# Scaled, newly split input as 512 moving columns in three FFN up projections, with accumulators in pairs of banks

## The chip, the cores and the metric

The kernel runs on one core of one Trainium2 chip. The metric is device time of one execution in microseconds (us). Three runs of the kernel before gave 1129.79 to 1129.9 us, median 1129.81. The profiled execution took 1131.31 us, of which the trace shows a span of 1129.5 us at a mean granted TensorE clock of 0.992.

## The reference

One sequence of 256 tokens (T), width 1024 (D_MODEL), goes through three mixing layers, each followed by a convolutional feed-forward network (FFN). The first mixing layer has three branches (an RWKV-7 recurrence, stick-breaking attention, attention to a memory) that a gate joins; the second and the third are other mixers. All is fp32. The change lies in the FFN and in where every accumulator is put:

```python
def rms_norm(x, g, eps=NORM_EPS):
    xf = x.astype(jnp.float32)
    y = xf * lax.rsqrt(jnp.mean(xf * xf, axis=-1, keepdims=True) + eps)
    return (y * g.astype(jnp.float32)).astype(x.dtype)

def conv_ffn(x, g, w_up, conv_w, conv_b, w_down):
    h = rms_norm(x, g) @ w_up                      # 1024 -> 2 x 2816
    ...
    acc = conv_b + hp[:, 0:t] * conv_w[0]          # causal, 3 taps over time
    for i in range(1, CONV_W):
        acc = acc + hp[:, i:i + t] * conv_w[i]
    gate, val = jnp.split(acc, 2, axis=-1)
    return (jax.nn.silu(gate) * val) @ w_down      # 2816 -> 1024
```

## The kernel before

Channels lie on the 128 partitions and the 256 tokens on the free axis, so x is eight tiles of 128x256 (k = 0 to 7, KD = 8), kept in `xt`. An fp32 product is made from three float32r products: each operand is split into a high part (a rounded copy, made by ACT) and a low part (what is left, a subtraction by DVE), and hi x hi, hi x lo and lo x hi are summed in PSUM. `mm3` (L365 to L367) issues the three for one 128x128 weight block: weight hi with moving Xh, weight hi with Xl, weight lo with Xh, 256 columns each.

Weights stream in tiles of 1024 columns, eight blocks each: a DMA on SP's queue into `wstg`, an ACT copy into `whi` (L241), a DVE subtraction into `wlo` (L242), three buffers of each. This goes on through the whole kernel.

The FFN input is X2 (X4, X6 in the other two): x times the norm's gain, split, but not yet divided by each token's root mean square. That factor (`s_bc`, 128x256, one value for each token) comes late: PE sums the squares (`st_ps`, L462), DVE moves the sum (L464), GpSimd takes the inverse root in eleven steps (L406 to L418), PE spreads it over the partitions (`st_pb`, L472), and ACT copies it out of PSUM (L474). The order of tokens and channels lets it be applied to the product instead of the input.

An up projection has 22 pairs (NJ = 22) of half-tiles, one for the gate and one for the value; each half-tile takes eight blocks. The first HEAD = 4 half-tiles run in two rounds, k = 0 to 5 for all, then k = 6 and 7. The rest run one after the other. A pair's two halves fill one bank, 128x512. `evac` then has DVE multiply the bank by `s_bc` into one of three `ffu` buffers (L1123), makes the causal convolution on ACT (L1127) and DVE (L1128, L1129), silu on ACT (L1131), the product on DVE (L1132), and splits the result into Y[j] (`ffy`, high and low side by side; L339, L340).

The down projection (`residual`, L1077 to L1089) has one accumulator of 128x512 for each of eight output tiles m: weight hi with the 512 columns [Yh, Yl] (L1083), weight lo with the 256 of Yh (L1085), over 22 blocks, then two DVE additions into `xt` (L1087).

Accumulators come from `ps_acc`: four buffers of one bank (128x512 fp32) that go round under the tag "acc". Gates and branches of the first mixer use one such bank for each m, the gate in the first 256 columns and the branch in the other 256 (L1035 to L1053); ACT takes tanh of the gate (L1037), DVE joins it with the branch (L1048, L1050, L1051). The projections of the RWKV branch take token-shifted sums from such banks with an ACT copy (L603) and a DVE operation (L605).

A scheduler that works on the program decides the order of instructions on each engine and places the waits; a wait is for the instructions that last read or wrote the same tile. Stages, by time in the profiled execution: first mixer to 344.7 us (its output projection `XO`, L1056 to L1058, from about 321), first FFN up 344.7 to 472, down 472 to 534; second mixer to 639, its FFN up to 766, down to 830; third mixer to 935, its FFN up to 1064, down to the end.

Of the kernel before, what the change touches and what calls it, by code (L numbers as in the profile page):

```python
# [16 lines left out]
T = 256  # L17
# [8 lines left out]

STARTS = (82, 148, 181, 247, 279)
GRID = 4
HEAD = 4

# [162 lines left out]
def body(tc, a, out, voff, coff, tap=None, upto=99):  # L195
# [8 lines left out]
    dpool = es.enter_context(tc.tile_pool(name="dpool", bufs=1, space=bass.MemoryType.DRAM))  # L204
    psum = es.enter_context(tc.tile_pool(name="psum", bufs=1, space=PSUM))

    def ps_acc(name="acc"):
        return psum.tile([128, 512], F32, name=name, tag="acc", bufs=4)

    def ps_m(name="pm"):  # L210
        return psum.tile([128, 512], F32, name=name, tag="pm", bufs=2)
# [110 lines left out]
    def vec(n, k=0, w=1):  # L322
        o = voff[n][0] + k
        return vecs[:, o:o + w]
# [67 lines left out]
                flow.tick(4)  # L392

    def tp_group(X):
        po = [ps_acc(), ps_acc()]
        tp_groups(X, po)
        return po

# [656 lines left out]
    def residual(X, gains_next, snext, Xn, kn=KD, two=False):  # L1055
# [10 lines left out]
                snext.add(xt[:, m - 1:m + 1])  # L1066

        if two:
            ps = [ps_acc() for _ in range(4)]
            for kh in range(2):  # L1070
                for m in range(KD):
                    o = ps[m // 2][:, m % 2 * T:(m % 2 + 1) * T]
                    for k in range(4 * kh, 4 * kh + 4):
                        mm3(o, X, k, W.take(), k == 0 and m % 2 == 0, k == kn - 1, skip_group_check=True)
                    if kh == 1 and m % 2 == 1:
                        evac(m - 1, 2, ps[m // 2].rearrange("p (j t) -> p j t", t=T))
        elif isinstance(X, list):  # L1077

            for m in range(KD):
                ps = ps_acc()  # L1080
                for k in range(kn):
                    hi, lo = W.take()
                    PE.matmul(ps, hi, X[k].rearrange("p s t -> p (s t)"), start=(k == 0), stop=False,  # L1083
                              skip_group_check=True)
                    PE.matmul(ps[:, 0:T], lo, X[k][:, 0], start=False, stop=(k == kn - 1), skip_group_check=True)  # L1085
                for j in range(2):
                    V.tensor_tensor(xt[:, m], xt[:, m], ps[:, (1 - j) * T:(2 - j) * T], op=OP.add)  # L1087
                after_tile(m)
        else:  # L1089
# [12 lines left out]
    order.close()  # L1102
    mix.close()

    def ffn(X, st, cname, gains_next, snext, Xn_f):
        fs = ExitStack()
        fp = fs.enter_context(tc.tile_pool(name="ffn_" + cname, bufs=1))
        Y = []
# [8 lines left out]
            G.memset(u[:, :, 0:2], 0.0)  # L1117
            ub.append(u)

        def evac(i, m, ps2):  # L1120
            j = i // 2
            u = ub[j % 3]
            V.tensor_tensor(u[:, :, 2:], ps2, st.bc2, op=OP.mult)  # L1123
            ac = fp.tile([128, 2, T], F32, name="ffa", bufs=3)
            for g in range(2):
                c = (j * 2 + g) * 4
# [275 lines left out]
```

## Time and profile before

| | before |
|---|---|
| median of the runs | 1129.81 us (1129.79 to 1129.9) |
| profiled execution / span | 1131.31 / 1129.5 us |
| PE busy | 1102.4 us (98%) |
| DVE busy | 869.5 us (77%) |
| ACT busy | 664.3 us (59%) |
| GpSimd busy | 64.1 us (6%) |
| HBM read | 186.46 MB, 166 GB/s over the span |

Busy time is the union of an engine's instructions over the span. A matmul's own duration, 0.28 us for 256 columns, overlaps the next ones; what one costs in a row of them is the distance between two starts. "Idle before, releaser" at a row is how long its engine stood still ahead of it, and what it waited for. In a row of instructions a bracket such as [waits DVE_49] says that it waits for a semaphore of that engine.

### The profile page before, as it was taken

How to read it: one execution, taken by the hardware profiler on the slowest of the kernel's cores; microseconds unless marked ns; L12 is line 12 of the kernel's file. 1: busy time of each engine (PE TensorE's matmuls, PEld its weight loads, DVE VectorE, ACT ScalarE, POOL GpSimd, SP SyncE). 2: the span in 40 equal slices, each digit the busy share in tenths (PEclk: the TensorE clock that was granted, in tenths of full speed). 3: DMA queues.
4: the chain of work that ended last, by engine and by line, in shares of the span. 5: the costliest groups of instructions: out<-in, count | busy, mean ns of one | idle time of the engine just before them, and what ended most of it. 6: DMA issues, size and time to landing. Idle time of an engine off the chain costs nothing.

```text
span 1129.5 us, 21212 instructions
## 1 busy us (share of the span) xinstructions
PE 1102.4 (98%) x8266; PEld 1027.4 (91%) x8266; DVE 869.5 (77%) x1615; ACT 664.3 (59%) x1116; POOL 64.1 (6%) x167
## 2 busy tenths in 40 slices
PE   7999989999999999999999999999999999999998
PEld 4898769899999999988989999998888899999987
DVE  6669875667676999966656889997779768999854
ACT  6556546654555666645546666665555756666642
POOL 2100210000011000000100110000010002000000
PEclk9899999999999999999999999999999999999999
DMA  7444333335475555566554565565665536655573
GB/s 278 162 132 149 114 113 103 95 96 150 150 225 173 183 187 187 181 189 196 168 169 149 164 193 189 181 180 182 195 200 175 165 94 190 181 181 183 185 208 110
DMA packets 60788, 189.28 MB, mean 168 GB/s; under 512 B 12688, under 2 KB 14992, under 8 KB 60688
## 3 DMA queue, kind: packets, MB, share of 16 engines
q1 hardware_dynamic: 59792, 186.51, 53.2%
q8 instruction: 65, 1.06, 0.4%
q0 software_dynamic: 320, 1.05, 0.3%
q10 hardware_dynamic: 576, 0.37, 0.1%
q14 instruction: 35, 0.29, 0.1%
HBM read 186.46 MB, written 1.44 MB: 166 GB/s over the span
## 4 chain that ended last, share of the span: by engine, by line
PE 87%; DVE 4%; DMA 3%; ACT 2%; SPq 1%; issue 1%; POOL 0%; DVEq 0%; ACTq 0%
PE acc L365 18%; PE acc L366 18%; PE acc L367 18%; PE acc L1083 11%; PE acc L1085 5%; PE acc L389 3%; PE acc L391 3%; PE acc L390 3%; DMA wstg<-in_wst_dram 2%; DVE wlo L242 1%; ACT whi L241 1%; PE rw_pp L811 1%; SPq L773 1%; DMA mst<-in_memT_dram 1%; PE rw_ps L706 0%
## 5 line engine op out<-in xcount | busy, mean ns | idle before, releaser
L241 ACT ACTIVATE whi<-wstg 128x1024 fp32r<-128x1024 f32 (+1 forms) x420 | 372.3, 903 | 330.5 <-PE acc L366 116.6
L242 DVE TENSOR_TENSOR wlo<-wstg,whi 128x1024 fp32r<-128x1024 f32 (+1 forms) x420 | 429.2, 1035 | 163.1 <-ACT whi L241 155.6
L1083 PE MATMUL acc<-ffy,whi 128*128 128x512 f32 x528 | 183.2, 395 | 0.0
L1085 PE MATMUL acc<-ffy,wlo 128*128 128x256 f32 x528 | 144.5, 278 | 0.0
L1083 PEld LDWEIGHTS acc<-ffy,whi 128*128 128x128 f32 x528 | 98.0, 188 | 22.0
L1085 PEld LDWEIGHTS acc<-ffy,wlo 128*128 128x128 f32 x528 | 99.3, 188 | 1.4
L366 PE MATMUL acc<-x6l,whi 128*128 128x256 f32 x352 | 99.3, 284 | 0.9 <-DVE x6l L343 0.9
L366 PE MATMUL acc<-x2l,whi 128*128 128x256 f32 x352 | 99.2, 283 | 0.0
L365 PE MATMUL acc<-x2h,whi 128*128 128x256 f32 x352 | 99.2, 283 | 0.0
L365 PE MATMUL acc<-x4h,whi 128*128 128x256 f32 x352 | 99.0, 283 | 0.0
L365 PE MATMUL acc<-x6h,whi 128*128 128x256 f32 x352 | 99.0, 283 | 0.0
L366 PE MATMUL acc<-x4l,whi 128*128 128x256 f32 x352 | 98.9, 283 | 0.0
L367 PE MATMUL acc<-x2h,wlo 128*128 128x256 f32 x352 | 97.8, 283 | 0.0
L367 PE MATMUL acc<-x4h,wlo 128*128 128x256 f32 x352 | 97.6, 283 | 0.0
L367 PE MATMUL acc<-x6h,wlo 128*128 128x256 f32 x352 | 97.6, 283 | 0.0
L365 PE MATMUL acc<-x1h,whi 128*128 128x256 f32 x304 | 89.6, 295 | 0.6 <-ACT x1h L546 0.6
L366 PE MATMUL acc<-x1l,whi 128*128 128x256 f32 x304 | 87.9, 289 | 1.9 <-DVE x1l L548 1.6
L367 PE MATMUL acc<-x1h,wlo 128*128 128x256 f32 x304 | 87.2, 287 | 0.0
L1127 ACT ACTIVATE ffa<-ffu,ffcv 128x256 f32<-128x256 f32 x132 | 70.7, 587 | 0.1
L366 PEld LDWEIGHTS acc<-x6l,whi 128*128 128x128 f32 x352 | 67.5, 192 | 1.3 <-DVE x6l L343 1.3
L365 PEld LDWEIGHTS acc<-x6h,whi 128*128 128x128 f32 x352 | 67.6, 192 | 0.0
L365 PEld LDWEIGHTS acc<-x2h,whi 128*128 128x128 f32 x352 | 67.6, 192 | 0.0
(612 smaller groups left out, 2665.2 us busy)
## 6 DMA issues: line engine op xcount, KB each, us to landing
wstg<-in_wst_dram SPq DMA_DIRECT2D x343, 512.0 KB, 3.6
wstg<-in_wst_dram SPq DMA_DIRECT2D x4, 256.0 KB, 5.9
mst<-in_memT_dram SPq DMA_DIRECT2D x4, 256.0 KB, 6.4
x<-in_xT_dram SPq DMA_DIRECT2D x2, 512.0 KB, 8.0
xt<-in_xT_dram POOLq DMA_DIRECT2D x4, 256.0 KB, 6.2
out_dram<-xt SPq DMA_DIRECT2D x8, 128.0 KB, 3.9
cst<-in_cst_dram SPq DMA_DIRECT2D x1, 673.0 KB, 4.8
small<-in_small_dram SPq DMA_DIRECT2D x1, 512.0 KB, 5.9
```

The source lines that it names most:

```text
L241: A.activation(hi[:, p], src[:, p], AF.Copy)
L242: V.tensor_tensor(lo[:, p], src[:, p], hi[:, p].bitcast(F32), op=OP.subtract)
L365: PE.matmul(o, hi, xh, start=start, stop=False, **kw)
L366: PE.matmul(o, hi, xl, start=False, stop=False, **kw)
L367: PE.matmul(o, lo, xh, start=False, stop=stop, **kw)
L389: PE.matmul(po[tt], X.H[:, k, s], hi, start=(k == 0), stop=False)
L390: PE.matmul(po[tt], X.L[:, k, s], hi, start=False, stop=False)
L391: PE.matmul(po[tt], X.H[:, k, s], lo, start=False, stop=(k == KD - 1))
L773: nc.sync.dma_start(X[h][r, :, j], dz[0, b, 8 * h:8 * h + 8].rearrange("u i j -> i u j"))
L1083: PE.matmul(ps, hi, X[k].rearrange("p s t -> p (s t)"), start=(k == 0), stop=False, skip_group_check=True)
L1085: PE.matmul(ps[:, 0:T], lo, X[k][:, 0], start=False, stop=(k == kn - 1), skip_group_check=True)
L1127: A.activation(ac[:, g], u[:, g, 2:], AF.Identity, scale=cv[:, c + 2:c + 3], bias=cv[:, c + 3:c + 4])
```

## The change

- HEAD goes from 4 to 6: the first six half-tiles keep the old form, with X2 and `s_bc` after the product.
- From the seventh half-tile on (j = 3 to 21) the moving operand is `Xs` (`ffx`): xt times gain times `s_bc` (one DVE operation for each k, L1163), split into high and low side by side (ACT copy L348, DVE subtraction L349). `mm3`'s first two matmuls become one of 512 columns (weight hi with [Xh, Xl], L1170), then weight lo with Xh (256 columns, L1171). The high and the low sums of a half-tile come out in different columns, 512 for each half-tile.
- `evac` of those pairs: ACT copies the low sums out of PSUM (`ffb`, L1136), and DVE adds the high sums to them (L1137), in place of the multiplication by `s_bc` (which stays for j = 0 to 2, L1133).
- Accumulators: two buffers of two banks in place of four of one. `ps_acc` hands out the two halves of one such tile one after the other, everywhere in the program.

```diff
-HEAD = 4
+HEAD = 6
...
-    def ps_acc(name="acc"):
-        return psum.tile([128, 512], F32, name=name, tag="acc", bufs=4)
+    halves = []
+
+    def ps_acc2(name="acc"):
+        halves.clear()
+        return psum.tile([128, 1024], F32, name=name, tag="acc", bufs=2)
+
+    def ps_acc():
+        if not halves:
+            t = ps_acc2()
+            halves.extend([t[:, 0:512], t[:, 512:1024]])
+        return halves.pop(0)
...
-        def evac(i, m, ps2):
-            j = i // 2
+        def evac(j, ps2, two):
             u = ub[j % 3]
-            V.tensor_tensor(u[:, :, 2:], ps2, st.bc2, op=OP.mult)
+            if two is None:
+                V.tensor_tensor(u[:, :, 2:], ps2, st.bc2, op=OP.mult)
+            else:
+                b_ = fp.tile([128, 2, T], F32, name="ffb", bufs=2)
+                A.activation(b_, two, AF.Copy)
+                V.tensor_tensor(u[:, :, 2:], ps2, b_, op=OP.add)
...
-        fp_pairs(X, 2 * NJ, evac, first=HEAD)
+                    evac(i // 2, ps[i // 2].rearrange("p (j t) -> p j t", t=T), None)
+            if ks[0] == 0:
+
+                Xs = fp.tile([128, KD, 2, T], F32R, name="ffx")
+                for k in range(KD):
+                    t_ = fp.tile([128, T], F32, name="ffxs", bufs=2)
+                    V.scalar_tensor_tensor(t_, xt[:, k], vec(gain, k), st.bc, op0=OP.mult, op1=OP.mult)
+                    split(Xs[:, k, 0], Xs[:, k, 1], t_)
+        for j in range(HEAD // 2, NJ):
+            ps = ps_acc2().rearrange("p (g s t) -> p g s t", g=2, s=2)
+            for g in range(2):
+                for k in range(KD):
+                    hi, lo = W.take()
+                    PE.matmul(ps[:, g], hi, Xs[:, k], start=(k == 0), stop=False, skip_group_check=True)
+                    PE.matmul(ps[:, g, 0], lo, Xs[:, k, 0], start=False, stop=(k == KD - 1), skip_group_check=True)
+            evac(j, ps[:, :, 0], ps[:, :, 1])
```

The scheduler moves instructions with it. Lines of the changed kernel below are 9 to 31 above those of before (L374 to L376 are `mm3`, L1093, L1095 and L1097 the down projection and its additions, L1142 and L1143 the convolution, L251 the weight split).

On PE, in the first mixer, the branch products of two gates that follow each other (`acc_3019` and `acc_3072` before, both in `acc_3004` after); before:

```order
L365 MATMUL acc_3019<-yB_1846,whi_3054 128x256
L366 MATMUL acc_3019<-yB_1846,whi_3054 128x256
L367 MATMUL acc_3019<-yB_1846,wlo_3055 128x256
L365 MATMUL acc_3072<-yB_1846,whi_3054 128x256 [waits Activation_49]
L366 MATMUL acc_3072<-yB_1846,whi_3054 128x256
L367 MATMUL acc_3072<-yB_1846,wlo_3055 128x256
L365 MATMUL acc_3072<-yB_1846,whi_3054 128x256
```

and after:

```order
L374 MATMUL acc_3004<-yB_1838,whi_3039 128x256
L375 MATMUL acc_3004<-yB_1838,whi_3039 128x256
L376 MATMUL acc_3004<-yB_1838,wlo_3040 128x256
L374 MATMUL acc_3004<-yB_1838,whi_3039 128x256 [waits DVE_49]
L375 MATMUL acc_3004<-yB_1838,whi_3039 128x256
L376 MATMUL acc_3004<-yB_1838,wlo_3040 128x256
L374 MATMUL acc_3004<-yB_1838,whi_3039 128x256
```

The second of them was in a bank of its own; now it writes the other half of the same tile, and its first matmul waits for DVE, by the resolved semaphores for L1060, which reads the branch whose last matmul stands one row above.

On PE at the head of the first FFN, around `st_pb`; before:

```order
L365 MATMUL acc_4146<-x2h_3627,whi_4066 128x256
L366 MATMUL acc_4146<-x2l_3628,whi_4066 128x256
L367 MATMUL acc_4146<-x2h_3627,wlo_4067 128x256
L365 MATMUL acc_4146<-x2h_3627,whi_4066 128x256
L472 MATMUL st_pb_4082<-cst_84,s2_rs_4089 128x128 [waits Pool_49]
L472 MATMUL st_pb_4082<-cst_84,s2_rs_4089 128x128
L366 MATMUL acc_4146<-x2l_3628,whi_4066 128x256
L367 MATMUL acc_4146<-x2h_3627,wlo_4067 128x256
```

and after:

```order
L376 MATMUL acc_3937<-x2h_3607,wlo_4043 128x256
L482 MATMUL st_pb_4090<-cst_84,s2_rs_4097 128x128 [waits Pool_49]
L482 MATMUL st_pb_4090<-cst_84,s2_rs_4097 128x128
L374 MATMUL acc_3936<-x2h_3607,whi_4042 128x256 [waits DVE_49]
L375 MATMUL acc_3936<-x2l_3608,whi_4042 128x256
L376 MATMUL acc_3936<-x2h_3607,wlo_4043 128x256
L374 MATMUL acc_3936<-x2h_3607,whi_4042 128x256
...
L1170 MATMUL acc_4228<-ffx_4088,whi_4072 128x512 [waits DVE_49,PE_49]
L1171 MATMUL acc_4228<-ffx_4088,wlo_4073 128x256
L1170 MATMUL acc_4228<-ffx_4088,whi_4072 128x512 [waits DVE_49]
...
L1170 MATMUL acc_4228<-ffx_4088,whi_4072 128x512 [waits DVE_49]
L1171 MATMUL acc_4228<-ffx_4088,wlo_4073 128x256
```

The x2 products went on across `st_pb` on a third accumulator; now what follows `st_pb` is in the second half of the first tile and waits for DVE's multiplication of the first half, and behind it the matmuls on `ffx` wait for the split of each k.

On DVE at the same place; before:

```order
L242 TENSOR_TENSOR wlo_4150<-wstg_4147,whi_4149 128x1024 [waits DMAHW0_49,PE_49,Activation_49]
L242 TENSOR_TENSOR wlo_4180<-wstg_4177,whi_4179 128x1024 [waits DMAHW1_49,PE_49,Activation_49]
L1123 TENSOR_TENSOR ffu0_3954<-acc_3960,s2_bc_4106 128x2x256 [waits Activation_49]
L1123 TENSOR_TENSOR ffu1_3956<-acc_3961,s2_bc_4106 128x2x256
L1123 TENSOR_TENSOR ffu2_3958<-acc_4146,s2_bc_4106 128x2x256 [waits PE_49]
L242 TENSOR_TENSOR wlo_4224<-wstg_4221,whi_4223 128x1024 [waits DMAHW2_49,Activation_49]
L1128 SCALAR_TENSOR_TENSOR ffa_4109<-ffu0_3954,ffcv_3952,ffa_4109 128x256 [waits Activation_49] x2
L1128 SCALAR_TENSOR_TENSOR ffa_4134<-ffu1_3956,ffcv_3952,ffa_4134 128x256 [waits Activation_49] x2
```

and after:

```order
L251 TENSOR_TENSOR wlo_4175<-wstg_4172,whi_4174 128x1024 [waits DMAHW1_49,PE_49,Activation_49]
L1163 SCALAR_TENSOR_TENSOR ffxs_4089<-xt_3602,vecs_83,s2_bc_4114 128x256 [waits Activation_49]
L1163 SCALAR_TENSOR_TENSOR ffxs_4119<-xt_3602,vecs_83,s2_bc_4114 128x256
L1133 TENSOR_TENSOR ffu0_3930<-acc_3936,s2_bc_4114 128x2x256
L1133 TENSOR_TENSOR ffu2_3934<-acc_3937,s2_bc_4114 128x2x256 [waits PE_49]
L349 TENSOR_TENSOR ffx_4088<-ffxs_4089,ffx_4088 128x256 [waits Activation_49]
...
L1133 TENSOR_TENSOR ffu1_3932<-acc_3936,s2_bc_4114 128x2x256 [waits PE_49]
L1143 SCALAR_TENSOR_TENSOR ffa_4160<-ffu0_3930,ffcv_3928,ffa_4160 128x256 [waits DVE_49]
...
L1163 SCALAR_TENSOR_TENSOR ffxs_4139<-xt_3602,vecs_83,s2_bc_4114 128x256 [waits DVE_49]
L1163 SCALAR_TENSOR_TENSOR ffxs_4143<-xt_3602,vecs_83,s2_bc_4114 128x256 [waits DVE_49]
...
L349 TENSOR_TENSOR ffx_4088<-ffxs_4139,ffx_4088 128x256 [waits Activation_49]
L349 TENSOR_TENSOR ffx_4088<-ffxs_4143,ffx_4088 128x256 [waits Activation_49]
L251 TENSOR_TENSOR wlo_4254<-wstg_4251,whi_4253 128x1024 [waits DMAHW3_49,PE_49,Activation_49]
```

Between the arrival of `s_bc` and the last part of `ffx` (the two rows on L349 ahead of `wlo_4254`) there are 36 rows, in which the eight scalings and eight subtractions alternate with the convolutions of the first three pairs.

On PE in the first down projection, where the output tiles m = 0 and m = 1 meet; before:

```order
L1083 MATMUL acc_5628<-ffy21_3951,whi_5631 128x512 [waits DVE_49]
L1085 MATMUL acc_5628<-ffy21_3951,wlo_5632 128x256
L1083 MATMUL acc_5695<-ffy18_3948,whi_5702 128x512 [waits Activation_49]
L1083 MATMUL acc_5764<-ffy0_3930,whi_5702 128x512 [waits PE_49]
L1085 MATMUL acc_5695<-ffy18_3948,wlo_5703 128x256 [waits DVE_49]
L1083 MATMUL acc_5695<-ffy19_3949,whi_5702 128x512
L1085 MATMUL acc_5695<-ffy19_3949,wlo_5703 128x256
...
L1083 MATMUL acc_5695<-ffy21_3951,whi_5702 128x512
L1085 MATMUL acc_5695<-ffy21_3951,wlo_5703 128x256
L1085 MATMUL acc_5764<-ffy0_3930,wlo_5703 128x256
L1083 MATMUL acc_5764<-ffy1_3931,whi_5702 128x512
```

and after:

```order
L1093 MATMUL acc_5370<-ffy19_3925,whi_5373 128x512
L1095 MATMUL acc_5370<-ffy19_3925,wlo_5374 128x256
L1093 MATMUL acc_5370<-ffy20_3926,whi_5373 128x512 [waits DVE_49]
L1095 MATMUL acc_5370<-ffy20_3926,wlo_5374 128x256
L1093 MATMUL acc_5370<-ffy21_3927,whi_5373 128x512 [waits DVE_49]
L1095 MATMUL acc_5370<-ffy21_3927,wlo_5374 128x256
L1093 MATMUL acc_5370<-ffy0_3906,whi_5373 128x512 [waits DVE_49]
L1095 MATMUL acc_5370<-ffy0_3906,wlo_5374 128x256
L1093 MATMUL acc_5370<-ffy1_3907,whi_5373 128x512
```

Before, m = 1 (`acc_5695`) and m = 2 (`acc_5764`) are banks of their own, and tile m = 1 was begun ahead of the last block of m = 0 (`acc_5628`); after, m = 0 and m = 1 are halves of `acc_5370`, and the first matmul of m = 1 waits for DVE's two additions that read m = 0.

## Rows read from the trace of the kernel before

**Rows 1.** The page: busy time of each engine, and the chain by engine.
```profile
PE 1102.4 (98%) x8266; PEld 1027.4 (91%) x8266; DVE 869.5 (77%) x1615; ACT 664.3 (59%) x1116; POOL 64.1 (6%) x167
...
PE 87%; DVE 4%; DMA 3%; ACT 2%; SPq 1%; issue 1%; POOL 0%; DVEq 0%; ACTq 0%
```

**Rows 2.** Stretches: window, length, busy PE, PEld, DVE, ACT, POOL, granted clock, DMA, GB/s.
```profile
47.00:321.00 274.00, 262.16 (x2304) 240.72 (x2303) 196.31 (x361) 155.32 (x259) 19.41 (x57) 0.98 0.42 126
...
344.00:472.00 128.00, 128.00 (x1070) 128.00 (x1069) 112.97 (x200) 82.37 (x135) 3.00 (x11) 1.00 0.58 181
```

**Rows 3.** Timeline of PE, up projection: start, duration, engine, line, op, out<-in, count.
```profile
346.18 0.28 PE L365 MATMUL acc<-x2h,whi 128*128 128x256 f32 x1
...
346.54 0.28 PE L365 MATMUL acc<-x2h,whi 128*128 128x256 f32 x1
```

**Rows 4.** Down projection's matmuls by tile: count, ns min/median/max, first and last start.
```profile
L1083 PE MATMUL acc<-ffy,whi x176: 389/395/404, 472.1 to 533.1; 128*128 128x512 f32 x176
```

**Rows 5.** Timelines of PE, GpSimd and DVE: the root mean square's way to the multiplication.
```profile
354.82 0.39 PE L462 MATMUL st_ps<-ones,st_acc 128*128 128x1 f32 x3
...
359.57 0.19 POOL L418 TENSOR_TENSOR s_rs<-s2w 128x2 f32<-128x2 f32 x1
...
361.50 0.38 PE L472 MATMUL st_pb<-cst,s_rs 128*128 128x128 f32 x2
...
362.33 1.89 DVE L1123 TENSOR_TENSOR ffu<-acc,s_bc 128x512 f32<-128x512 f32 x3 [0.35 <-ACT s_bc L474]
```

**Rows 6.** By tile: scaling of x, the FFN's convolution and split, weight splits.
```profile
L544 DVE SCALAR_TENSOR_TENSOR x<-x,vecs,s_bc x8: 478/480/485, 33.8 to 42.7; 128x256 f32<-128x256 f32 x8
...
L1128 DVE SCALAR_TENSOR_TENSOR ffa<-ffu,ffcv,ffa x132: 476/480/494, 365.3 to 1069.2; 128x256 f32<-128x256 f32 x132
...
L340 DVE TENSOR_TENSOR ffy<-fft,ffy x66: 416/418/434, 374.7 to 1073.4; 128x256 fp32r<-128x256 f32 x66
...
L241 ACT ACTIVATE whi<-wstg x420: 398/1060/1066, 3.7 to 1116.8; 128x1024 fp32r<-128x1024 f32 x107, 128x256 fp32r<-128x256 f32 x33
```

**Rows 7.** Timelines: last up product on PE; last pair's split on DVE; ACT's 512-column copy.
```profile
471.98 0.28 PE L367 MATMUL acc<-x2h,wlo 128*128 128x256 f32 x1
...
481.84 0.43 DVE L340 TENSOR_TENSOR ffy<-fft,ffy 128x256 fp32r<-128x256 f32 x1 [0.48 <-ACT ffy L339]
...
37.14 0.69 ACT L526 ACTIVATE mv<-acc,sm_rs 128x512 f32<-128x512 f32 x1
```

**Rows 8.** Timeline of DVE in the down projection: additions and weight splits.
```profile
486.35 0.88 DVE L1087 TENSOR_TENSOR xt<-xt,acc 128x256 f32<-128x256 f32 x2 [1.22 <-PE acc L1085]
487.14 1.22 DVE L242 TENSOR_TENSOR wlo<-wstg,whi 128x1024 fp32r<-128x1024 f32 x1
488.28 0.42 DVE L1087 TENSOR_TENSOR xt<-xt,acc 128x256 f32<-128x256 f32 x1
```

**Rows 9.** Timelines: PE finds a DVE result; DVE adds PE's last product.
```profile
38.64 0.39 PE L366 MATMUL acc<-x1l,whi 128*128 128x256 f32 x1 [0.37 <-DVE x1l L548]
...
38.17 0.42 DVE L548 TENSOR_TENSOR x1l<-x,x1h 128x256 fp32r<-128x256 f32 x1
...
344.62 0.28 PE L367 MATMUL acc<-xoh,wlo 128*128 128x256 f32 x1
...
344.94 0.42 DVE L1058 TENSOR_TENSOR xt<-xt,acc 128x256 f32<-128x256 f32 x1 [0.51 <-PE acc L367]
```

**Rows 10.** By tile: the evacuations of the first mixer.
```profile
L1037 ACT ACTIVATE gt<-acc x24: 363/383/386, 174.5 to 316.9; 128x256 f32<-128x256 f32 x24
L1050 DVE SCALAR_TENSOR_TENSOR gt<-gt,acc x16: 412/416/422, 252.7 to 321.2; 128x256 f32<-128x256 f32 x16
...
L603 ACT ACTIVATE rw_m<-acc,vecs x14: 455/458/476, 49.3 to 95.7; 128x256 f32<-128x256 f32 x14
```

**Rows 11.** PE after an idle time in the first mixer: timeline, then the stretch.
```profile
131.47 1.09 PE L946 MATMUL me_t<-cst,me_p 128*128 128x128 f32 x4 [2.27 <-DVE me_p L931]
...
131.40:134.40 3.00, 2.93 (x9) 2.60 (x10) 1.19 (x5) 0.60 (x1) 1.29 (x7) 0.50 0.48 175
```

More of the change, by code (lines that the diff above doesn't have):

```diff
@@ L394, in tp_group @@
     def tp_group(X):
-        po = [ps_acc(), ps_acc()]
+        t = ps_acc2()
+        po = [t[:, 0:512], t[:, 512:1024]]
         tp_groups(X, po)
@@ L1068, in residual @@
         if two:
-            ps = [ps_acc() for _ in range(4)]
+            ps = [t[:, h * 512:(h + 1) * 512] for t in (ps_acc2(), ps_acc2()) for h in range(2)]
             for kh in range(2):
@@ L1103, in body, with ffn @@
     mix.close()
-    def ffn(X, st, cname, gains_next, snext, Xn_f):
+    def ffn(X, st, gain, cname, gains_next, snext, Xn_f):
         fs = ExitStack()
@@ L1133, in evac @@
             split(Y[j][:, 0], Y[j][:, 1], th)
+        halves.clear()
         ps = [ps_acc() for _ in range(HEAD // 2)]
@@ L1141, in ffn @@
                 if ks[-1] == KD - 1 and i % 2:
-                    evac(i - 1, 2, ps[i // 2].rearrange("p (j t) -> p j t", t=T))
-        fp_pairs(X, 2 * NJ, evac, first=HEAD)
+                    evac(i // 2, ps[i // 2].rearrange("p (j t) -> p j t", t=T), None)
[13 more added lines that the diff above has]
+            evac(j, ps[:, :, 0], ps[:, :, 1])
         Xn = Xn_f()
@@ L1149, in body @@
     s3 = Stats("s3", G)
-    X3, = ffn(X2, s2, "conv0", ["a_norm"], s3, lambda: [Pair("x3", "ab")])
+    X3, = ffn(X2, s2, "norm2_g", "conv0", ["a_norm"], s3, lambda: [Pair("x3", "ab")])
     dbg("b1", xt)
@@ L1283, in body @@
     s5 = Stats("s5", G)
-    XQ, XK = ffn(X4, s4_, "conv1", ["b_norm", "kv_norm"], s5, lambda: [Pair("xq", "de"), Pair("xk", "ab")])
+    XQ, XK = ffn(X4, s4_, "f_norm0", "conv1", ["b_norm", "kv_norm"], s5, lambda: [Pair("xq", "de"), Pair("xk", "ab")])
     dbg("b2f", xt)
@@ L1368, in body @@
     mix.close()
-    ffn(X6, s6, "conv2", [], None, lambda: [])
+    ffn(X6, s6, "f_norm1", "conv2", [], None, lambda: [])
     for k in range(KD):
```

## Prediction

> **What bounds the kernel now.** I read the busy times first: TensorE (PE) is busy for 1102.4 of 1129.5 us, and 87% of the chain that ends last is PE's [rows 1]. So only two things count: how long PE takes for its matmuls, and whether it waits. The stretches come next: in the FFN's up projection PE never stands still (128.00 of 128 us), and DVE has some room (112.97 us); in the first mixer PE idles 12 of 274 us, and DVE is busy for 196 [rows 2]. From the timelines and tiles I then took how long a handed-over result takes, since the order of the changed kernel shows many more waits of PE for an evacuation. A change of 0.2% (2.3 us) is about what a measurement can tell from none.
>
> **The matmuls.** Before, a block of an up projection takes three starts at 0.12 us: 0.360 us [rows 3]. The form with 512 + 256 columns runs in the down projection: 175 steps between the first and last of 176 blocks in 533.1 - 472.1 = 61.0 us, 0.3486 us each [rows 4]. The gain is 0.0114 us a block; 38 half-tiles of 8 blocks in each of three FFNs are 912 blocks: **-10.4 us**.
>
> The Trainium skill ("TensorE: Matmul & The Clock Gate", section "Wait — 56ns, not 53.3ns?") has N / 2.4 GHz plus about 2.5 ns between starts: an estimate of 327.5 ns for three of 256 columns and 325 for 512 + 256, thus 2.3 us over 912 blocks. These rows run slower than that in both forms, so the sum goes by the rows.
>
> **In the steady state of the up projection** the new work is hidden. A pair takes PE 16 x 0.3486 = 5.58 us. DVE pays per pair two weight splits, one addition of 512 columns, four convolution steps, a product and a subtraction. Between starts DVE needs 0.08 us less than a duration (a split of 1.22 takes 1.14 from start to start [rows 8]): 2 x 1.14 + 0.60 + 4 x 0.40 + 2 x 0.34 = 5.2 us, 0.60 being a third of the 1.89 us for three of 512 columns, less 0.08 [rows 5, 6]. That is what DVE did before with a multiplication in the addition's place. ACT gains a copy of 512 columns (0.69 us [rows 7]), and has room: 59% busy [rows 1]. The tile with two banks is wanted again a whole pair later, and copy and addition end some 2 us after its last matmul. Cost: nothing.
>
> **The head of each FFN.** Here the scaled input has to be made, and PE has too little to do meanwhile. I count from `st_ps`, when PE sums the squares. The inverse root is there 4.94 us later (354.82 to 359.57 + 0.19), and DVE could use `s_bc` 0.83 us after `st_pb` started (361.50 to 362.33) [rows 5]. Before, PE came to `st_pb` only after 53 rows, so it did not wait. Now 24 matmuls (2.9 us) stand between: PE waits there for 2.0 us, and `s_bc` is with DVE at 4.94 + 0.06 + 0.83 = 5.83. From there to the last subtraction for `ffx`, DVE has 8 scalings at 0.40, 8 subtractions at 0.34, three multiplications at 0.60, 12 convolution steps at 0.40, three products and three subtractions at 0.34 and a weight split of 1.14 [rows 5, 6, 8]: 15.7 us. So k = 7 is ready at 21.6. PE's work up to that wait is 24 + 12 matmuls at 0.12 (the 12 finish j = 1 and wait for DVE's read of the other half), `st_pb` at some 0.2, and 14 pairs at 0.3486, since the scheduler draws in six pairs of j = 4: 9.4 us. **PE loses 12.3 us.** This counts DVE's work alone. If DVE also waits 0.4 us, the length of an ACT operation of 256 columns [rows 10], at each of the eight k, it is 15.5; if half of the 12 convolution steps don't stand in the way, 9.9.
>
> The granted clock falls on top. After PE had idled 2.27 us, its clock stood at 0.50 for 3 us [rows 11]: 1.5 us lost. In the head there are several waits of that order, close together; I count it once. 13.8 us for each FFN, three of them: **+41.4 us** (bounds 30 and 51).
>
> **Half-tiles.** The order keeps its waits by tile, so a matmul into the second half of a two-bank tile waits for the reads of the first. In the changed kernel 33 waits of PE for an evacuation have at most 0.6 us between the last product that is read and the matmul that waits (counting matmuls by 0.12); before there was none, the least had 1.26. What such a wait costs: from the start of the last product 0.28 to its end, 0.04 to DVE's start (344.90 to 344.94), 0.42 for an operation of 256 columns, 0.05 to PE's start (38.59 to 38.64), and that matmul takes 0.22 instead of 0.12 to the next start, less the 0.12 that would have passed anyway [rows 9]: 0.77 us. A weight split that stands in front on DVE makes it 1.90 with its 1.14 [rows 8].
>
> The Trainium skill would have it otherwise ("PSUM — Partial Sum Buffer", section "Summary: rules for kernel authors"): reading while a matmul runs wants a different bank, and semaphores by bank. By that the halves, each a bank, need no wait; that is the first rival below. The order's rows show the wait by tile, and no run here has shown its price yet.
>
> - First mixer: eight zero-slack waits for DVE in the gates at 1.34, midway between 0.77 and 1.90: 10.7. Three for ACT's tanh, with a weight copy queued in front: 0.28 + 0.04 + 0.98 + 0.38 + 0.05 + 0.10 - 0.12 = 1.7 each, 5.1 [rows 6, 9, 10]. Three in the token shift, where ACT and DVE each take two operations in turn (0.46 and 0.48 [rows 6, 10]): 1.8 when they overlap, 2.4 when not, 2.1 each, 6.3. Seven gates with 1.44 us of room against 1.7: 1.8. Sum **+23.9** (bounds 13 and 34). Idle time of PE that is there already [rows 2] may swallow a part.
> - Output projection of the first mixer: three waits at 1.34: **+4.0** (2.3 and 5.7).
> - Down projections: m = 1, 3, 5, 7 wait for both additions of the m before. Two in a row make 0.77 + 0.40 = 1.16 [rows 8, 9]; at m = 3 and 7 a weight split stands between them: 2.3. That is 6.9 for each FFN. Ahead of it, m = 0 can no longer be left open while m = 1 starts: before, Y's last part was ready 10.3 us after the last up product began (471.98 to 482.27), with three weight splits in between. PE has 21 blocks, 7.3 us, until it needs that part. Without any split in the way the chain is some 6 us and costs nothing; with all, and ACT's new 0.69, it is 11.0 and costs 3.7 [rows 7]. I take the middle, 1.8. So 8.7 x 3 = **+26.1** (14 and 38).
> - Second and third mixer: two waits for a 512-column evacuation at about 1.4, and three small ones, 1.5 together: **+4.3** (2 and 6).
>
> **Sum.** -10.4 + 41.4 + 23.9 + 4.0 + 26.1 + 4.3 = **+89.3 us**. On the profiled execution's 1131.31 us (a span of 1129.5 and 1.8 around it) that gives 1220.6; the runs' median lies 1.5 below that execution, so 1219 us.
>
> **The rivals.**
>
> *The halves don't cost.* If the reads end in time, or the waits stand where PE waits anyway, the terms of the half-tiles fall away but for the one at the last part of Y: -10.4 + 41.4 + 5.4 = +36, 1166 us. For it: 98% busy PE leaves evacuations mostly early, and DVE is idle 23% of the time [rows 1]. Against it: at zero slack even an idle DVE takes 0.77 us.
>
> *The clock falls after the short waits too.* The waits of 2.1 to 2.3 us in the down projections (six) and in the shift (three) are near the 2.27 us after which the clock was at 0.50 [rows 11]: nine times 1.5, +13.5: 1233 us. Against it, that wait is the only one of its length here to go by.
>
> *Faster.* If the weights' scheduler room and DVE's idle time take in the splits of `ffx` as well, only the matmuls are left: 1129.8 - 10.4 = 1119.4 us. It decides at one place: the last k of `ffx` would have to be ready before PE's 9.4 us after `st_ps` are over, though `s_bc` alone is there at 5.83 and eight scalings and eight subtractions take 5.9. Even with all else of DVE put behind, 2.3 us would be missing, so this is hardly possible. A 512-column matmul that gains nothing here, on the other hand, would only add 10 us to the forecast.
>
> **How the numbers follow.** Forecast 0.68; the halves cost little 0.13; the clock falls more often 0.14; only the matmuls count 0.02; what remains, 0.03, goes to sums between. The bounds of the terms add to about +51 and +124, that is 1181 and 1254. Taking both rivals in part, the range is 1172 to 1252. Faster by over 0.2%: 0.03, from the third rival and a little for what I have not seen; no change 0.02; slower 0.95.
>
> **What would show it.** In the profile after: `st_pb` with an idle time of about 2 us ahead of it, and matmuls on `ffx` that wait for DVE, some 12 us in each head, followed by a stretch of granted clock 0.5; 512-column matmuls in the up projection 0.3486 us a block and no idle time from j = 6 on; idle times of 1.1 to 2.3 us on PE ahead of m = 1, 3, 5 and 7 of each down projection, released by `xt`; idle times of 0.8 to 1.9 us in the gates. PE's busy time would fall by some 10 us, and its idle time rise from 27 to about 120. I am wrong if the up projections show waits throughout (DVE or ACT as the bound), if the waits between halves are near zero, or if a down projection takes 61 us as before.

## The result, and the profile after

The changed kernel takes 1240.14 us (median of four runs, 1236.49 to 1241.17) against 1129.86 us: slower, a ratio of 1.097 with a 95% interval of 1.095 to 1.099. The forecast was 1219 us with a range of 1172 to 1252. The profiled execution has a span of 1234.4 us, 105 us more than before.

The page's first part, busy time of each engine, to set beside [rows 1]:

```profile
PE 1128.1 (91%) x7354; PEld 999.2 (81%) x7354; DVE 890.4 (72%) x1663; ACT 706.1 (57%) x1197; POOL 64.1 (5%) x167
```

PE is idle for 106 us where it was idle for 27. Its busy time rises too, by 26 us, although 912 matmuls went away. One reason is the clock: its mean in the profiled execution is 0.970, before 0.992, so PE did more of its work at the lower of the two levels (0.50, that is 1.2 of 2.4 GHz). The other three runs stand at 0.965 to 0.967 and took 3.3 to 4.7 us longer than the profiled one. The table places the 105 us. A stage runs from the first matmul of its tile to that of the next.

| stage | before | after | difference | forecast |
|---|---|---|---|---|
| start and first mixer | 321.0 | 355.9 | +34.9 | +23.9 |
| output projection, first up projection | 151.1 | 163.7 | +12.6 | +14.3 |
| second / third up projection | 127.4 / 128.8 | 136.0 / 137.1 | +8.7 / +8.4 | +10.3 each |
| down projections (the last with the end) | 61.4, 61.4, 65.8 | 72.7, 72.4, 76.8 | +11.3, +11.1, +11.0 | +8.7 each |
| second and third mixer | 105.8, 106.9 | 111.9, 107.9 | +6.1, +1.0 | +4.3 |

The list of PE's waits, in the view that groups them by line and releaser (total, times, longest), names the changed kernel's new ones:

```profile
PE acc L1093 <- DVE xt L1097: 17.8, 12, 2.0
PE acc L374 <- DVE rw_krv L615: 10.2, 2, 6.5
PE acc L1170 <- DVE ffx L349: 7.9, 9, 2.5
PE acc L374 <- DVE macc L1058: 7.1, 3, 3.0
PE acc L1093 <- DVE ffy L349: 6.4, 3, 2.1
PE st_pb L482 <- POOL s_rs L428: 6.1, 4, 1.8
PE acc L374 <- DVE ffu L1133: 6.0, 3, 2.0
PE acc L374 <- ACT gt L1047: 5.7, 4, 1.5
PE acc L374 <- DVE gt L1060: 5.1, 6, 1.2
...
PE acc L374 <- DVE rw_wl L615: 3.8, 1, 3.8
```

The twelve waits for `xt` are m = 1, 3, 5, 7 of the three down projections, the three for `ffy` the last part of Y ahead of them. `gt`, `macc`, `rw_krv` and `rw_wl` are the first mixer's halves. `ffx`, `ffu` and three of the four waits at `st_pb` are the FFN heads. None of these lines is among PE's waits before.

The head of the first FFN, on PE's timeline (start, duration, what; in brackets the idle time in front and its releaser):

```profile
395.33 0.50 PE L472 MATMUL st_ps<-ones,st_acc 128*128 128x1 f32 x4
...
400.59 0.43 PE L482 MATMUL st_pb<-cst,s_rs 128*128 128x128 f32 x2 [1.77 <-POOL s_rs L428]
403.01 0.58 PE L374 MATMUL acc<-x2h,whi 128*128 128x256 f32 x1 [1.99 <-DVE ffu L1133]
...
408.38 0.58 PE L1171 MATMUL acc<-ffx,wlo 128*128 128x256 f32 x1 [0.66 <-DVE wlo L251]
...
414.69 0.50 PE L1170 MATMUL acc<-ffx,whi 128*128 128x512 f32 x1 [2.53 <-DVE ffx L349]
...
417.50 0.79 PE L1170 MATMUL acc<-ffx,whi 128*128 128x512 f32 x1 [0.49 <-DVE ffx L349]
```

The last wait for `ffx` ends 22.2 us after `st_ps` (20.8 us in the second and the third FFN); DVE's queue was forecast to end at 21.6. The stretches (window, length, busy PE, PEld, DVE, ACT, POOL, granted clock, DMA, GB/s) show the clock in the head, and the steady state that follows:

```profile
404.00:405.70 1.70, 1.70 (x10) 1.70 (x9) 1.70 (x5) 0.08 (x1) 0.00 (x0) 0.50 0.00 0
405.70:412.00 6.30, 5.64 (x18) 4.09 (x16) 5.98 (x14) 6.01 (x11) 0.00 (x0) 0.50 0.25 83
...
417.40:420.00 2.60, 2.50 (x11) 2.17 (x12) 0.38 (x2) 0.66 (x1) 0.00 (x0) 0.72 0.00 0
...
425.00:519.50 94.50, 94.50 (x546) 83.65 (x546) 89.70 (x155) 72.46 (x121) 0.00 (x0) 1.00 0.59 195
```

After the first two waits the clock stands at its lower level. It costs little there: PE does at half speed, while it would have to wait for DVE anyway, what it would otherwise have done before a longer wait. It is low once more behind the last wait, where it does cost time: 0.72 over 2.60 us, 0.7 us. From 425 us on PE is never idle. By the tile's own view (count, ns min/median/max, first and last start) 271 steps take 94.0 us:

```profile
L1170 PE MATMUL acc<-ffx,whi x272: 390/390/480, 425.2 to 519.2; 128*128 128x512 f32 x136
```

That is 0.3469 us a block, 0.0131 less than the three-matmul form [rows 3]: the gain is there, 912 x 0.0131 = 12 us.

The down projection, on PE's timeline:

```profile
529.14 0.50 PE L1093 MATMUL acc<-ffy,whi 128*128 128x512 f32 x1 [2.14 <-DVE ffy L349]
530.72 0.50 PE L1093 MATMUL acc<-ffy,whi 128*128 128x512 f32 x1 [0.97 <-DVE xt L1097]
549.79 0.50 PE L1093 MATMUL acc<-ffy,whi 128*128 128x512 f32 x1 [1.98 <-DVE xt L1097]
...
566.61 0.50 PE L1093 MATMUL acc<-ffy,whi 128*128 128x512 f32 x1 [1.01 <-DVE xt L1097]
...
584.39 0.50 PE L1093 MATMUL acc<-ffy,whi 128*128 128x512 f32 x1 [1.98 <-DVE xt L1097]
```

Idle time leaves out the last matmul's 0.28 us, of which 0.12 would have passed anyway, and the 0.10 that the first one after a wait takes longer: 0.97 and 1.98 us of idle cost 1.2 and 2.2, against the forecast's 1.16 and 2.3. Behind the two waits that follow each other the clock falls, behind a single one of 1.98 us it stays up:

```profile
531.00:535.00 4.00, 4.00 (x15) 3.44 (x15) 1.71 (x2) 1.26 (x2) 0.00 (x0) 0.57 0.03 3
549.70:552.00 2.30, 2.21 (x12) 1.94 (x13) 0.52 (x2) 0.51 (x1) 0.00 (x0) 1.00 0.65 214
```

So it is in all three down projections of this execution, but not in every run. With the pairs alone (the first experiment below), three of six single waits of some 2 us were followed by the lower level, for instance:

```profile
857.68 0.50 PE L1093 MATMUL acc<-ffy,whi 128*128 128x512 f32 x1 [1.98 <-DVE xt L1097]
```

```profile
859.20:862.60 3.40, 3.40 (x13) 2.92 (x12) 0.99 (x1) 1.06 (x1) 0.00 (x0) 0.50 0.32 128
```

In the run without the factor it was two of six. What decides it there is open.

### The profile page after: what moved, and what is told of

Same layout as the page of the kernel before. It is cut to its first block, busy times and chain, and to the rows that moved or that the text cites. A ratio compares the mean times of both kernels' runs of the same rounds, so it can differ in the third digit from the quotient of the medians.

```text
span 1234.4 us, 19498 instructions
## 1 busy us (share of the span) xinstructions
PE 1128.1 (91%) x7354; PEld 999.2 (81%) x7354; DVE 890.4 (72%) x1663; ACT 706.1 (57%) x1197; POOL 64.1 (5%) x167
## 5 line engine op out<-in xcount | busy, mean ns | idle before, releaser
L251 DVE TENSOR_TENSOR wlo<-wstg,whi 128x1024 fp32r<-128x1024 f32 (+1 forms) x420 | 429.2, 1035 | 218.3 <-ACT whi L250 213.8
L1170 PE MATMUL acc<-ffx,whi 128*128 128x512 f32 x912 | 328.1, 401 | 8.6 <-DVE ffx L349 7.9
L1171 PE MATMUL acc<-ffx,wlo 128*128 128x256 f32 x912 | 262.1, 287 | 1.1 <-DVE wlo L251 0.9
L1170 PEld LDWEIGHTS acc<-ffx,whi 128*128 128x128 f32 x912 | 176.0, 193 | 50.4 <-DVE ffx L349 12.1
L1093 PE MATMUL acc<-ffy,whi 128*128 128x512 f32 x528 | 191.4, 405 | 24.2 <-DVE xt L1097 17.8
L1171 PEld LDWEIGHTS acc<-ffx,wlo 128*128 128x128 f32 x912 | 177.3, 194 | 2.6 <-DVE wlo L251 2.6
L1095 PE MATMUL acc<-ffy,wlo 128*128 128x256 f32 x528 | 149.6, 283 | 0.0
L1093 PEld LDWEIGHTS acc<-ffy,whi 128*128 128x128 f32 x528 | 101.3, 192 | 52.6 <-DVE xt L1097 21.6
L374 PE MATMUL acc<-x1h,whi 128*128 128x256 f32 x304 | 93.8, 308 | 26.9 <-DVE rw_krv L615 10.2
L1095 PEld LDWEIGHTS acc<-ffy,wlo 128*128 128x128 f32 x528 | 101.8, 193 | 0.0
L376 PE MATMUL acc<-x1h,wlo 128*128 128x256 f32 x304 | 89.3, 294 | 0.0
L374 PEld LDWEIGHTS acc<-x1h,whi 128*128 128x128 f32 x304 | 61.8, 203 | 31.2 <-DVE rw_krv L615 10.6
L375 PEld LDWEIGHTS acc<-x1l,whi 128*128 128x128 f32 x304 | 62.0, 204 | 2.6 <-DVE x1l L558 2.4
L376 PEld LDWEIGHTS acc<-x1h,wlo 128*128 128x128 f32 x304 | 61.9, 204 | 0.0
L1142 DVE SCALAR_TENSOR_TENSOR ffa<-ffu,ffcv,ffa 128x256 f32<-128x256 f32 x132 | 58.1, 479 | 0.1
L1143 DVE SCALAR_TENSOR_TENSOR ffa<-ffu,ffcv,ffa 128x256 f32<-128x256 f32 x132 | 58.1, 478 | 0.0
L374 PE MATMUL acc<-x3h,whi 128*128 128x256 f32 x136 | 39.9, 294 | 0.4 <-ACT whi L250 0.4
L376 PE MATMUL acc<-x3h,wlo 128*128 128x256 f32 x136 | 39.6, 291 | 0.8 <-DVE wlo L251 0.8
```

The costliest lines, as they stand in the source:

```text
L251: V.tensor_tensor(lo[:, p], src[:, p], hi[:, p].bitcast(F32), op=OP.subtract)
L374: PE.matmul(o, hi, xh, start=start, stop=False, **kw)
L375: PE.matmul(o, hi, xl, start=False, stop=False, **kw)
L376: PE.matmul(o, lo, xh, start=False, stop=stop, **kw)
L1142: V.scalar_tensor_tensor(ac[:, g], u[:, g, 1:T + 1], cv[:, c + 1:c + 2], ac[:, g], op0=OP.mult, op1=OP.add)
L1143: V.scalar_tensor_tensor(ac[:, g], u[:, g, 0:T], cv[:, c:c + 1], ac[:, g], op0=OP.mult, op1=OP.add)
```

## The experiments

Theory A: two things cost, waits between the halves of a two-bank tile, everywhere in the program, and DVE's queue behind the token factor in each FFN head. Theory B: the pairs of banks are harmless, and the changed FFN's load on DVE and ACT delays the rest.

**Pairs of banks alone.** Before, with the change's `ps_acc2`, `ps_acc` and no other part of it:

```diff
-        fp_pairs(X, 2 * NJ, evac, first=HEAD)
+        for i in range(HEAD, 2 * NJ, 2):
+            pj = ps_acc2()[:, 0:512]
...
```

> The kernel before with one part of the change alone: accumulators as pairs of banks, handed out in halves, everywhere as in the change (the FFN's up projection keeps its three 256-column products and takes a tile of its own for each pair, of which it uses one half). Theory A (half-tile waits): the stages outside the FFN heads lose what they lost in the changed kernel: first mixer +34.9 us, output projection about +3, down projections 11.3 + 11.0 + 10.8, second and third mixer 6.1 + 1.0, so about +75 and 1205 us (1185 to 1220). Theory B (the down projections and the first mixer lose because the changed FFN loads DVE and ACT and moves their work): the pairs alone cost little, 1130 to 1150 us, and the down projections take 61 to 63 us.

Measured 1221.93 us, ratio 1.079 (1.076 to 1.082): +91 us, 2 us above the expected range. The first mixer's length is 356.1 us (355.9 in the changed kernel), the down projections 73.3, the second mixer 110.6. Its waits, by the same view, are the changed kernel's:

```profile
PE acc L1093 <- DVE xt L1097: 18.1, 12, 2.2
PE acc L374 <- DVE rw_krv L615: 10.2, 2, 6.5
PE acc L374 <- DVE ffu L1133: 8.0, 3, 2.7
PE acc L374 <- DVE macc L1058: 7.1, 3, 3.0
```

B falls: without any of the FFN's new work the same lines wait for the same time. What I had left out is the third line: the old head pays for halves too, and the second and third up projection take 3.0 and 4.2 us longer.

**The change without the pairs.** Four accumulators of one bank; a half-tile has its own:

```diff
-            ps = ps_acc2().rearrange("p (g s t) -> p g s t", g=2, s=2)
+            ps = [ps_acc().rearrange("p (s t) -> p s t", s=2) for _ in range(2)]
```

> The changed kernel without pairs: four accumulators of one bank; a half-tile of the up projection with its 512 columns has a bank of its own, and its evacuation is two copies and two additions of 256 columns in place of one each of 512. Theory A: first mixer, down projections and the other mixers fall back to the times of before, and the heads remain: 1130 - 10 for the matmuls + 3 x 12.2 for the heads = 1156 us (1140 to 1165; the heads may lose less, since PE can go on in a second bank while the first is read). Theory B: 1200 us or more.

Measured 1153.76 us, ratio 1.020 (1.018 to 1.022), as A has it. First mixer 320.1 us, the first two down projections 61.2 each, other mixers within 0.3 us of before. The up projections stay long (135.3 and 136.7), and their waits are the head's:

```profile
PE acc L1160 <- DVE ffx L340: 12.7, 7, 4.5
PE acc L1160 <- issue: 9.0, 2, 4.5
```

The second line names no releaser ("issue"); its two waits stand where the first head has its wait of 4.5 us for `ffx`.

The pairs alone cost 91 us and the rest of the change alone 23, 114 together; the whole change costs 109 against the same runs of before. So the two parts nearly add.

**The factor left out of the split input.**

```diff
-                    V.scalar_tensor_tensor(t_, xt[:, k], vec(gain, k), st.bc, op0=OP.mult, op1=OP.mult)
+                    V.tensor_scalar(t_, xt[:, k], vec(gain, k), None, op0=OP.mult)
```

> The changed kernel with the split input scaled by the gain alone; the token factor is left out of the pairs from j = 3 on, so the split input can be made before the factor is known. Theory A (the head loses because eight scalings, copies and subtractions queue on DVE behind the factor): of the 12.2 us that each FFN's up projection lost beyond its matmuls, only the wait for the first pair's multiplication stays, about 2 to 4 us: 1240 - 3 x 9 = 1213 us (1205 to 1222). Rival (the head loses by the amount of DVE work there, whenever it may start): the same instructions on DVE, 1235 to 1240 us.

Measured 1224.2 us, ratio 1.082 (1.079 to 1.084): 16 us less than the changed kernel, not 27, and 2 us outside the range. No wait for `ffx` is left, so the queue behind the factor was what these waits came from. (The scaling also becomes a shorter operation without the factor, 0.35 us for 0.48, some 1 us of DVE's work in each head, which is not told apart.) But the wait at `st_pb` grows, as PE comes to it after 12 matmuls in place of 24, and the wait for `ffu` only shrinks from 6.0 to 3.6:

```profile
PE st_pb L482 <- POOL s_rs L428: 9.7, 4, 3.4
...
PE acc L374 <- DVE ffu L1133: 3.6, 3, 1.2
```

The 12.6 us that a head loses are therefore not a sum of separate waits: with the splits out of the queue, the factor's way through GpSimd and the wait for the other half still hold 7 to 8 us, which the splits had covered. By stages the three up projections are 6.7, 4.6 and 5.1 us shorter than in the changed kernel; the first mixer (+2.9) and the last two down projections (+1.8, +2.1), which this edit does not touch, are longer, with more of their time at the lower clock (each of the two down projections has 3.4 us more at 0.50).

**Whole tiles in two places.** In the RWKV projections and the down projections only:

```diff
-            ps = ps_acc()
+            ps = ps_acc2()[:, 0:512]
```

> The changed kernel, in which the RWKV branch's shifted projections and the down projections take a whole two-bank tile for each accumulator and use one half, so that nothing waits for the other half; two buffers then go round. Theory A: each down projection comes back from 72.5 to 61 to 64 us (-9 to -11 each; the wait for the last part of Y may stay at 2 us), and the first mixer loses its three waits of 3.76, 3.76 and 6.48 us and the slow clock behind them, -12 to -18 us: 1240 - 30 - 15 = 1195 us (1185 to 1205). Rival (DVE is late there anyway, by its queue): waits of the same length move to the next use of a buffer, 1225 to 1240 us.

Measured 1187.26 us, ratio 1.049 (1.048 to 1.051). The first two down projections take 61.8 us each, the first mixer 340.5 (-15.4); PE has no wait left in these down projections, `rw_wl` is gone, `rw_krv` keeps 0.9. A holds, the rival does not: in the two places no wait moves to a later use of the buffer. Elsewhere, where nothing was edited, two waits grow a little (`ffx` from 7.9 to 10.6 us, `macc` from 7.1 to 8.5).

**Input split early, factor afterwards.** One-bank accumulators, HEAD = 4, and the factor applied to the sum, on GpSimd or on DVE (`V` in place of `G`). Against the change without the pairs:

```diff
-HEAD = 6
+HEAD = 4
...
                     V.tensor_tensor(u[:, g, 2:], ps2[g], b_[:, g], op=OP.add)
+                    G.tensor_tensor(u[:, g, 2:], u[:, g, 2:], st.bc, op=OP.mult)
...
-                    t_ = fp.tile([128, T], F32, name="ffxs", bufs=2)
-                    V.scalar_tensor_tensor(t_, xt[:, k], vec(gain, k), st.bc, op0=OP.mult, op1=OP.mult)
-                    split(Xs[:, k, 0], Xs[:, k, 1], t_)
+                    split(Xs[:, k, 0], Xs[:, k, 1], xt[:, k], vec(gain, k))
```

> Accumulators of one bank; four half-tiles of head in the old form; from the fifth on 512 moving columns of an input that is split with the gain alone, ready before the factor; ACT copies the low sums, DVE adds the high ones, and GpSimd multiplies by the token factor in SBUF (256 columns at a time), so that nothing of the computation is left out. Theory A: neither half-tile waits nor a queue behind the factor are left, so the matmuls' gain shows: 40 half-tiles x 8 x 3 = 960 blocks at 0.0114 us, -10.9: 1120 us, or up to 1130 if the head waits for a bank (a pair now takes two of the four banks while the factor is on its way). Rival (the gain in the matmuls is an appearance, given back by work that DVE and ACT gain): 1131 us or more, with waits all along the up projection.

> The same with DVE in GpSimd's place for the multiplication. DVE's work for a pair becomes about 5.2 + 2 x 0.34 = 5.9 us against PE's 5.58, so DVE would be the bound of the up projection: 20 pairs x 3 x 0.3 = 18 us above the version with GpSimd, some 1138 us; if the estimate of DVE's work for a pair is 0.3 us too high, it comes out even with it.

Measured 1161.42 us with GpSimd (ratio 1.027, 1.026 to 1.029), a miss of 31 us beyond the 1130, and 1139.99 with DVE (1.008, 1.007 to 1.010), near the 1138 of DVE as the bound; but that was to be 18 us above the version with GpSimd, and it is 21 below. With GpSimd the second step of the convolution and the split of Y grow on DVE; by tile, with GpSimd and then with DVE (ns min/median/max):

```profile
L1135 DVE SCALAR_TENSOR_TENSOR ffa<-ffu,ffcv,ffa x132: 470/667/965, 367.2 to 1102.3; 128x256 f32<-128x256 f32 x132
...
L340 DVE TENSOR_TENSOR ffy<-fft,ffy x66: 405/954/964, 378.2 to 1106.9; 128x256 fp32r<-128x256 f32 x66
```

```profile
L1135 DVE SCALAR_TENSOR_TENSOR ffa<-ffu,ffcv,ffa x132: 465/472/486, 369.3 to 1086.4; 128x256 f32<-128x256 f32 x132
```

So the move takes 49 us of multiplications (120 of 0.41) from DVE, and these two lines alone cost DVE 47 us more (89.7 for 62.2, 46.8 for 27.2). DVE's busy time is 929.1 us with GpSimd and 917.3 with all of it on DVE. With GpSimd it is busy for all of the 90 us from 380 to 470: it was the bound, and was not relieved.

**Low part by GpSimd.** The change without pairs, and the subtraction for `ffx` on GpSimd (with four temporary tiles `ffxs` in place of two):

```diff
-                    t_ = fp.tile([128, T], F32, name="ffxs", bufs=2)
+                    t_ = fp.tile([128, T], F32, name="ffxs", bufs=4)
...
-                    split(Xs[:, k, 0], Xs[:, k, 1], t_)
+                    A.activation(Xs[:, k, 0], t_, AF.Copy)
+                    G.tensor_tensor(Xs[:, k, 1], t_, Xs[:, k, 0].bitcast(F32), op=OP.subtract)
```

> The change with one-bank accumulators, where GpSimd instead of DVE subtracts for the low part of the scaled input (with four temporary tiles in place of two). If DVE's queue behind the factor bounds the head, 8 x 0.34 = 2.7 us go from it and each head loses that much less: 1154 - 8 = 1146 us (1143 to 1150). Rival (the head is bound by the time at which the factor arrives and by PE's banks): 1153 to 1156 us. A slow subtraction on GpSimd would make it longer instead.

Measured 1149.95 us, ratio 1.017 (1.016 to 1.018): 4 us less than without it, half of what was expected, at the end of the range. PE now waits for GpSimd's subtraction (9.9 us in three waits), which takes 0.88 us instead of 0.42. That the head follows who makes `ffx` is shown; the size of DVE's share is not told apart from GpSimd's slower work and the two additional tiles.

**512 columns only from pair 10 or 13 on.** One-bank accumulators; each of pairs 2 to 9 keeps three matmuls and asks for one k of the scaled input:

```diff
+        for j in range(HEAD // 2, 10):
...
+                fp_tile(pj[:, g * T:(g + 1) * T], X)
...
+            k = j - HEAD // 2
+            if k < KD:
...
+                V.scalar_tensor_tensor(t_, xt[:, k], vec(gain, k), st.bc, op0=OP.mult, op1=OP.mult)
+                split(Xs[:, k, 0], Xs[:, k, 1], t_)
```

> Accumulators of one bank and the change's scaled, newly split input, but the 512-column form only from pair j = 10 on; j = 2 to 9 keep three 256-column products with the factor after the product, and one k of the scaled input is asked for with each of those pairs, so that DVE makes it in the room that the old form leaves it. Theory A (the matmul gain is real, and what ate it in the one-bank version of the change was only the queue behind the factor): 12 pairs x 16 x 3 = 576 blocks at 0.0114 us, -6.6: 1131 - 6.6 = 1124.5 us (1123 to 1127), the first version faster than before. Rival (any 8 x 0.74 us more of DVE work behind the factor delays PE, since DVE is nearly full in this stage): 1131 to 1140 us, with waits for DVE in pairs 2 to 10.

> The same with the 512-column form from j = 13 on. Theory A: 9 x 16 x 3 = 432 blocks, -4.9: 1126 us, 1.6 us above the version from j = 10. Rival: if DVE's work delays PE in the version from j = 10, this one has three more pairs to catch up and is the faster of the two.

Measured 1127.43 us from pair 10 on (ratio 0.9973, 0.9964 to 0.9982) and 1129.88 from pair 13 on (0.9996, 0.9987 to 1.0006). The first is faster than the kernel before by 0.3%, 3.2 us, about half of the 6.6 expected; the second cannot be told from before, where 4.9 us were expected. Its rival, by which the later start would be the faster, falls too. The 512-column stretch is full, and DVE nearly so:

```profile
343.70:403.50 59.80, 59.38 (x490) 58.81 (x489) 51.92 (x99) 39.68 (x69) 3.00 (x11) 1.00 0.51 168
403.50:469.80 66.30, 66.30 (x385) 58.77 (x384) 65.20 (x125) 50.39 (x95) 0.00 (x0) 1.00 0.61 198
```

The up projections of the profiled execution are 1.1 to 1.4 us shorter each, where 2.5 (192 x 0.0131) were to be had. The 512-column stretch keeps its rate (0.347 us a block), so what is missing lies in the stretch ahead of it, into which the splits were put: a wait of 0.42 us for a weight split, some 0.7 with end and refill, is part of it; the rest I did not trace.

## Why the prediction was right, and where not

- **Matmuls, -10.4:** right, 12 by the rows of after. The estimate of 2.3 us from the spacing in the Trainium skill ("TensorE: Matmul & The Clock Gate", section "Wait — 56ns, not 53.3ns?") would have been far too small.
- **Heads, +41.4:** right in mechanism (the last k 22.2, 20.8 and 20.8 us after `st_ps`, forecast 21.6). Measured 8.7 and 8.4 plus the matmuls' 4.0 make 12.6 and 12.4 for the second and third, against 13.8. Mis-sized is the clock put on top: most of the time at 0.50 lies inside the wait, and only what is left behind the last wait, 0.7 us in the first head, is added in place of 1.5. (The terms before the clock, as written, also add to 12.1 and not 12.3.) The experiment without the factor shows that the waits here overlap.
- **Half-tiles in the down projections, +26.1:** each wait has its forecast price. Measured +33.4, since behind two waits in succession (2.14 and 0.97 us of idle) the clock is at 0.57 over 4 us, 1.7 us each time; and the wait for Y's last part costs 2.4 with end and refill, where I had 1.8. The rival that put the clock behind each wait of some 2 us does not hold in the profiled execution, where it stayed up behind six single waits of 1.98 us. It is not refuted for all runs: with the pairs alone it fell behind three of six.
- **First mixer, +23.9:** near for the gates: 17.9 us of idle in 13 waits (`macc`, `gt` on ACT and on DVE), 21 with the matmul's end and refill, forecast 17.6. Mis-sized in the shift, 6.3 us for waits that show 3.76, 3.76 and 6.48, 14.8 in all with end and refill. And the shift takes longer by more than its waits. From the first product on `x1h` to the first matmul on `rw_sc` PE issues 335 matmuls in both kernels; before and after:

```profile
37.28 0.28 PE L365 MATMUL acc<-x1h,whi 128*128 128x256 f32 x1
...
85.07 0.38 PE L706 MATMUL rw_ps<-rw_sc,rw_bk 64*128 64x128 f32 x2
```

```profile
34.94 0.28 PE L374 MATMUL acc<-x1h,whi 128*128 128x256 f32 x1
...
100.35 0.38 PE L716 MATMUL rw_ps<-rw_sc,rw_bk 64*128 64x128 f32 x2
```

  That is 47.8 and 65.4 us, +17.6 (47.4 us with whole tiles in that place). The 2.8 us beyond the waits fit PE's work at the lower clock behind each of the three, which the forecast had only in a rival; after the first, second and third:

```profile
50.00:52.00 2.00, 2.00 (x13) 2.00 (x12) 0.00 (x0) 0.77 (x2) 0.00 (x0) 0.55 0.53 207
...
68.00:70.00 2.00, 2.00 (x11) 2.00 (x11) 0.00 (x0) 0.10 (x1) 0.00 (x0) 0.50 0.38 152
...
90.00:92.00 2.00, 2.00 (x9) 2.00 (x10) 0.00 (x0) 0.42 (x1) 0.00 (x0) 0.50 0.00 0
```

  The mixer behind the shift takes 19.6 us longer, and all ahead of it 2.3 us less, which makes the 34.9. The source of the miss: I counted ACT's and DVE's four operations and forgot what stands between them on DVE. DVE's timeline ahead of the last wait:

```profile
85.97 0.47 DVE L615 SCALAR_TENSOR_TENSOR rw_krv<-acc,pre,rw_m 128x256 f32<-128x256 f32 x1
86.37 0.41 DVE L690 TENSOR_TENSOR rw_sc<-rw_f 64x256 f32<-64x256 f32 x1
...
89.01 0.42 DVE L693 TENSOR_TENSOR rw_bk<-rw_f 64x256 f32<-64x256 f32 x1
89.46 0.48 DVE L615 SCALAR_TENSOR_TENSOR rw_krv<-acc,pre,rw_m 128x256 f32<-128x256 f32 x1
```

  Eight operations of the recurrence stand between the two reads that PE waits for, 3.1 us.
- **Output projection and other mixers, +8.3:** close; three waits of 2.4 us of idle in all, 3.2 with end and refill, and +7.1. The rival in which the halves cost nothing (1166 us) is refuted by the run with the pairs alone.
- **The sum:** of the 21 us between 1219 and 1240, 11 are the shift and 7 the down projections; the heads give 3 back. Some 5 come from setting the median 1.5 us below the profiled execution, as before: it lies 3.7 above it, and the other runs have the lower mean clock. PE's busy time was to fall by 10 us and its idle time to rise to about 120; it rose by 26, and the idle time came to 106: in the heads part of the wait went into work at the lower clock.

## What to carry to other kernels

Where dependencies are kept by tile, a tile that spans two banks is one buffer, not two: before merging accumulators, look for every place in the program where the second half is written while the first is read, and price it with the whole queue of the engine that reads it, not with that engine's one operation. Count what PE does at a lower clock behind long waits as a cost of its own, and expect it to differ from run to run. A factor that arrives late is cheap when applied to the product and dear when an operand has to be made behind it; make such an operand in the slack of work that does not need it. A gain of 3.6% in a matmul's form, here 1% of the time, is undone by twelve waits of a microsecond.

## What was not expected of the hardware

A GpSimd operation on 128x256 values from SBUF stretches a DVE operation with two inputs from SBUF that starts during it. On the timelines of the version with the factor on GpSimd, GpSimd's and then DVE's:

```profile
424.89 0.82 POOL L1129 TENSOR_TENSOR ffu<-ffu,s_bc 128x256 f32<-128x256 f32 x1 [2.56 <-DVE ffu L1128]
```

```profile
424.74 0.47 DVE L1134 SCALAR_TENSOR_TENSOR ffa<-ffu,ffcv,ffa 128x256 f32<-128x256 f32 x1
425.13 0.86 DVE L1135 SCALAR_TENSOR_TENSOR ffa<-ffu,ffcv,ffa 128x256 f32<-128x256 f32 x1
```

The DVE operation that had begun first keeps its 0.47 us, the next one begins at 425.13 and ends at 425.99, 0.28 us after GpSimd's, 0.39 longer than alone. The Trainium skill ("SBUF — State Buffer", section "SBUF: two separate sides") says that a DVE operation with two SBUF inputs and a GpSimd operation that reads SBUF exclude each other, and that the one that starts first keeps the shared ports until it ends; these rows agree.

A mean granted clock is not a time by itself: the profiled execution without pairs shows 0.95 throughout its down projections, which take 61.2 us, where they took 61.4 at 1.00 before.
